# Splitting the projection matmuls of a two-layer hybrid trunk into halves of 256 columns

## The chip, the cores and the metric

The kernel runs on one core of a Trainium2 chip. The metric is the device time of one execution in microseconds (us). A core has a matrix engine (TensorE; PE in the profile, its weight loads PEld), a vector engine (DVE), a scalar engine (ACT), GpSimd (POOL) and a sync engine (SP) that issues most of the transfers.

## What is computed

512 tokens of 1,024 features pass two layers. Each layer normalizes its input, projects it to a wide row (queries, keys, values, gate), mixes the tokens, multiplies by the gate and projects back:

```python
for i in range(2):
    mod = silu(c) @ ada_w[i] + ada_b[i]
    shift, scale, gate = split(mod, 3)
    h = rms_norm(x, norm_g[i]) * (1 + scale) + shift
    if i == 0:   # retention, 4 heads; w_in is 1024 x 6144
        q, k, v, g = split(h @ ret_w_in, ...)
        o = rms_norm(retention(rope(q), rope(k), v)) * silu(g)
        out = o @ ret_w_out
    else:        # chunked attention, 16 heads; w_in is 1024 x 8192
        q, k, v, g = split(h @ att_w_in, 4)
        o = attention(rms_norm(q), rms_norm(k), v, bias) * silu(g)
        out = o @ att_w_out
    x = x + gate * out
```

The arithmetic is float32. The kernel gets it from TensorE with three products: each operand is split into a high and a low part, and high x high, high x low and low x high are summed.

## The kernel before, in words

**Input projections.** A `Chunk` (L290) is 512 columns of `w_in` (256 in one case at the start). Its weights come in two halves of 512 rows: `load` (L248) transfers them to `raw`, and ACT and DVE split them into `whi` and `wlo`. `Chunk.unit` then issues, for 128 tokens or 128 features and one half of the rows, 4 k-tiles of 3 matmuls into one PSUM tile `pm_...`; the second half ends the sum, and `evac` takes it. There are two forms:

- `nat_mm` (L270): the activations `hT` are the stationary operand (128 columns of it), 512 columns of weights stream past; L275 to L277. Used for `pm_rv` (values of layer 0), `pm_aqk` (queries and keys of layer 1) and `pm_av` (values). The output projections `po_r` and `po_a` use it as well.
- `tr_mm` (L279): the weights are stationary and 512 tokens of `hT` stream past; L283 to L285. Used for `pm_rqk`, `pm_rg` and `pm_ag` (queries and keys of layer 0, the gates).

A PSUM tile holds 128 x 512 float32. Every matmul of the program loads its stationary operand itself.

**Other products.** The scores `st` (L586, layer 0) and `as` (L787, layer 1) and the mixings `ro` (L606) and `ao` (L827) have 512, 384 or 256 columns, since later tokens see more keys; those of 256 are whole matmuls, not halves. A mixing block has twelve matmuls, three of 512, three of 384 and six of 256. Transposes (`hp`, `qt`, `pt`, `ss`) and column sums (`mod`) have 128 columns or one.

**The order.** Products run as units of 12 matmuls, one after the other in the order of the `go(...)` calls; scores, transposes, mixings and the adaLN sums of the next layer (`acc`, L150, on DVE) are hung behind given units with `at`. A planner in the framework sets the final order of each engine by simulated times. At the start (L386 to L464) the adaLN vectors of layer 0 are built from their weights by quarters, and the first products run beside that, k-tiles at a time.

Of the kernel before, what the change touches and what calls it, by code (L numbers as in the profile page):

```python
# [17 lines left out]
P = 128  # L18
S = 512
# [23 lines left out]
def hybrid_trunk_kernel(  # L43
# [71 lines left out]
    def rstd_of(ss, n, w):  # L115
        """ss [P, w] sums of squares over n -> (ss / n + eps) ** -0.5."""
        ms = sp.tile([P, w], F32, tag="ms", name="ms")
        nc.gpsimd.tensor_scalar(ms, ss, 1.0 / n, EPS, ALU.mult, ALU.add)
        rs = sp.tile([P, w], F32, tag="rs", name="rs")
        nc.gpsimd.tensor_tensor(rs, ms, mhalf[:, :w], ALU.pow)  # L120
        return rs

# [1 line left out]
    def ada_load(pool, layer, col, half):  # L124
# [9 lines left out]
    def ada_acc(pool, layer, col):  # L134
        """sum over k-tiles of cond * ada_w on every partition: [P, 512], in two steps;
        a gate's bias stands in the sum of the first partition."""
        acc = np_.tile([P, 512], F32, tag="acc", name=f"acc_{layer}_{col}", bufs=1)
        gate = col >= 2 * D
        if gate:
            nc.gpsimd.memset(acc, 0.0)  # L140
            nc.gpsimd.dma_start(acc[0:1, :], ada_b[layer : layer + 1, col : col + 512])
        for half in range(2):
            raw = ada_load(pool, layer, col, half)
            for k in range(4):
                kt = half * 4 + k
                c1 = cond[:, kt : kt + 1]
                if kt == 0 and not gate:
                    nc.vector.tensor_scalar(acc, raw[:, k, :], c1, None, ALU.mult)
                else:
                    nc.vector.scalar_tensor_tensor(acc, raw[:, k, :], c1, acc, ALU.mult, ALU.add)  # L150
            if half == 0:
                yield
        yield acc

    def column_sums(blocks, name, direct=False):
        """blocks: lists of [P, P]; the sums over their partitions, as [P, blocks]."""
        n, z = len(blocks), len(blocks[0])
        if direct:
            ps = pa.tile([P, n], F32, tag="pa", name=name)
            for j, parts in enumerate(blocks):  # L160
                for i, a in enumerate(parts):
                    mm = nc.tensor.matmul(
                        ps[:, j : j + 1], a, ones[:, 0:1], start=i == 0, stop=i == z - 1
                    )
            return ps, mm
        ps = pa.tile([P, n, z * P], F32, tag="pa", name=name)
        for j, parts in enumerate(blocks):
            for i, a in enumerate(parts):
                mm = nc.tensor.transpose(ps[:, j, i * P : (i + 1) * P], a, ident)
        sums = sp.tile([P, n], F32, tag=f"sums{n}", name=f"sums_{name}")  # L170
        nc.vector.tensor_reduce(sums, ps, mybir.AxisListType.X, ALU.add)
        return sums, mm

    def ada_finish(layer, col, accs, n):
        """n * 128 columns of scale or shift, summed over the partitions and laid over them."""
        c0 = col // P
# [12 lines left out]
    def ada(pool, layer, col):  # L189
        """512 columns: scale and shift laid over the partitions, the gate on each of them."""  # L190
        for acc in ada_acc(pool, layer, col):
# [13 lines left out]

# [1 line left out]
    def norm_rows(t, tag, scalar=False):  # L207
        """x / rms(x), in two halves of the columns."""
        xn, ss = [], sp.tile([P, 2], F32, tag="ss", name=f"ss_{tag}_{t}")
# [36 lines left out]

# [1 line left out]
    def load(parts, name, width=512, scale=None, w=None, k0=0, k1=4, low=None):  # L248
        """k-tiles k0..k1 of a piece of 4; parts: (columns of the tile, rows of the weights)."""
        if w is None:  # L250
# [18 lines left out]

    def nat_mm(ps, ah, al, tsl, w, kt0, first, last, ks=range(4)):  # L270
        """ps[tok, 512] += a[k, tok]^T w[k, 512]: ah/al(k) give the activations."""
        _, wh, wl = w
        for k in ks:
            a_h, a_l = ah(kt0 + k)[:, tsl], al(kt0 + k)[:, tsl]
            nc.tensor.matmul(ps, a_h, wh[:, k, :], start=first and k == 0, stop=False)  # L275
            nc.tensor.matmul(ps, a_h, wl[:, k, :], start=False, stop=False)  # L276
            nc.tensor.matmul(ps, a_l, wh[:, k, :], start=False, stop=last and k == 3)  # L277

    def tr_mm(ps, csl, w, kt0, first, last, ks=range(4)):  # L279
        _, wh, wl = w  # L280
        for k in ks:
            h, l = hT["h"][:, kt0 + k, :], hT["l"][:, kt0 + k, :]
            nc.tensor.matmul(ps, wh[:, k, csl], h, start=first and k == 0, stop=False)  # L283
            nc.tensor.matmul(ps, wh[:, k, csl], l, start=False, stop=False)  # L284
            nc.tensor.matmul(ps, wl[:, k, csl], h, start=False, stop=last and k == 3)  # L285

# [3 lines left out]
    class Chunk:  # L290
        """Columns of an input projection; cols: list of (columns of the tile, first column)."""

# [15 lines left out]
        def unit(self, half, u, ks=range(4)):  # L308
            if half == 0 and ks[0] == 0:
                self.ps.append(  # L310
                    self.pool.tile([P, 512], F32, tag=self.tag, name=f"pm_{self.name}_{u}")
                )
            sl = slice(u * P, (u + 1) * P)
            if self.transposed:
                tr_mm(self.ps[u], sl, self.w, half * 4, half == 0, half == 1, ks)
            else:
                nat_mm(self.ps[u], hh, hl, sl, self.w, half * 4, half == 0, half == 1, ks)
            if half == 1 and ks[-1] == 3:
                self.evac(u, self.ps[u])
# [10 lines left out]

    # Products run as units of 12 matmuls; the other work is hung behind given units.
    now = [0]
# [52 lines left out]

# [1 line left out]
    new_h(0)  # L387
# [5 lines left out]
    with tc.tile_pool(name="st", bufs=1) as st:  # L393
# [42 lines left out]
        def prepare(s, behind=None):  # L436
            """features 256 * s.. of h, and their rows of the first weights."""
            ada_256(D + s * 256, "scale", s == 0, behind)
# [29 lines left out]
    def probabilities(pool):  # L468
        """key tiles j on the partitions, their queries from tile j on; the last one is
        given the tile before it, as zeros."""  # L470
        pth = pool.tile([P, 1408], F32R, name="pth")
# [6 lines left out]

    # ================= layer 0: retention =================
    with ExitStack() as l0:  # L480
# [116 lines left out]
        def mix(n, f):  # L597
            """a block of 128 features of head n: products, gate and gain; the mean square waits."""
            ps = pa.tile([P, 512], F32, tag="pa", name=f"ro_{n}_{f}")
# [18 lines left out]
            nc.vector.tensor_tensor(y, ps, gg[n, f], ALU.mult)  # L618
            # the last head takes the place of the queries and keys, which are done with
            a, b = ("yh", "yl") if n < 3 else (("qh", "ql"), ("kh", "kl"))[f % 2]  # L620
# [9 lines left out]
        def norm_y(n):  # L630
            """1 / rms of head n for each token, on the partitions."""
            ps, _ = column_sums([[rstd[n][:, t * P : (t + 1) * P]] for t in range(NT)], f"ss_{n}")
# [61 lines left out]
        new_h(1)  # L694
        # the first weights of layer 1 take the place of the last values
        early = Chunk("aqk0", att_w_in, qk_cols(0), False, None)
# [7 lines left out]

    # ================= layer 1: chunked attention =================
    with ExitStack() as l1:
# [5 lines left out]
        def do_qk(b, begun=None):  # L712
            """heads 2b, 2b + 1."""
            nat = []
# [120 lines left out]
        def finish(h):  # L835
# [4 lines left out]
            else:  # L840
                if not last_y:
                    # the last heads take the place of the layer's input
                    last_y["h"] = hp.tile([P, NK, S], F32R, tag="hTh", name="yh_last")
# [5 lines left out]
        def hang(h, a, b, c, d=0):  # L849
            """behind units: a the scores, b the transposes, c the mixing."""  # L850
            at(a - 3, bias, h)
# [46 lines left out]
def _constants():  # L898
    """Tables that depend on shapes alone: rope frequencies and retention decays."""
    inv = np.array([int(v, 16) for v in _INV_FREQ_HEX.split()], dtype=np.uint32).view(np.float32)  # L900
# [66 lines left out]
```

## Time and profile before

| | |
|---|---|
| time, median of 2 runs | 999.24 us (996.72 and 1,001.76) |
| span of the profiled execution | 996.1 us |
| TensorE matmuls | 963.9 us busy (97%), 4,572 instructions |
| TensorE weight loads | 803.9 us (81%), 4,572 instructions |
| DVE | 608.7 us (61%) |
| ACT | 384.3 us (39%) |
| POOL | 212.1 us (21%) |
| DMA | 111.26 MB, mean 112 GB/s |

The span runs from the first to the last instruction of one profiled execution. Busy time is the union of the records of an engine; matmul records overlap, so a listed duration is longer than the distance between the starts of two neighbours. "Releaser" is what ended an idle time.

### The profile page before, as it was taken

The numbers are of one execution on the slowest core, as the hardware profiler recorded it, in microseconds if no ns is written. First come the engines' busy times: TensorE is split into PE (matmuls) and PEld (weight loads), VectorE is DVE, ScalarE is ACT, GpSimd is POOL, SyncE is SP. The second block draws the span as 40 slices with busy tenths as digits, with TensorE's granted clock in tenths as the row PEclk, the third lists the DMA queues.
The fourth block names the chain that finished last, engine by engine and source line by source line (L and its number), as shares of the span: only waits on it lengthen the run. The fifth ranks groups of instructions, "written<-read, shape, count | busy, mean of one in ns | idle before, by whom it ended". The sixth has DMA issues, their size and how long they took to land.

```text
span 996.1 us, 11965 instructions
## 1 busy us (share of the span) xinstructions
PE 963.9 (97%) x4572; PEld 803.9 (81%) x4572; DVE 608.7 (61%) x1012; ACT 384.3 (39%) x813; POOL 212.1 (21%) x205
## 2 busy tenths in 40 slices
PE   4999979999999999999999999999999999999988
PEld 3778868888778888888788888888888888888876
DVE  6977789558862563766445566545556346556683
ACT  6433413232223333426344445234543244444431
POOL 4810231004200103612100270002520012004520
PEclk8799989999999999999999999999999999999999
DMA  9645534653262222222232222223223232213202
GB/s 336 215 129 188 180 126 129 193 196 124 89 209 98 85 85 84 85 85 85 93 104 71 74 96 96 96 85 93 73 78 97 84 96 90 90 56 99 91 1 85
DMA packets 80537, 111.26 MB, mean 112 GB/s; under 512 B 12016, under 2 KB 44832, under 8 KB 80480
## 3 DMA queue, kind: packets, MB, share of 16 engines
q1 hardware_dynamic: 68368, 102.77, 31.3%
q0 software_dynamic: 10960, 5.63, 2.1%
q10 hardware_dynamic: 1152, 2.10, 0.6%
q8 instruction: 36, 0.59, 0.2%
q14 instruction: 21, 0.17, 0.1%
HBM read 108.32 MB, written 2.10 MB: 111 GB/s over the span
## 4 chain that ended last, share of the span: by engine, by line
PE 81%; DVE 8%; DMA 5%; issue 3%; POOL 1%; ACT 1%; SPq 0%; POOLq 0%; DVEq 0%; ACTq 0%
PE pm_aqk L277 6%; PE pm_aqk L275 6%; PE pm_aqk L276 6%; PE ao L827 3%; PE as L787 3%; PE pm_av L276 3%; PE pm_av L277 3%; PE pm_av L275 3%; PE po_a L277 3%; PE po_a L276 3%; PE po_a L275 3%; PE pm_ag L283 3%; DVE acc L150 3%; PE pm_ag L284 3%; PE pm_ag L285 3%; DMA ada<-in_ada_w_dram 3%
## 5 line engine op out<-in xcount | busy, mean ns | idle before, releaser
L275 PE MATMUL pm_aqk<-whi_aqk,hTh 128*128 128x512 f32 x256 | 101.8, 398 | 0.0
L277 PE MATMUL pm_aqk<-whi_aqk,hTl 128*128 128x512 f32 x256 | 100.5, 393 | 0.0
L276 PE MATMUL pm_aqk<-wlo_aqk,hTh 128*128 128x512 f32 x256 | 100.3, 392 | 0.0
L150 DVE SCALAR_TENSOR_TENSOR acc<-ada,cond,acc 128x512 f32<-128x512 f32 x60 | 52.9, 882 | 22.5 <-DMA ada<-in_ada_w_dram 11.5
L275 PE MATMUL pm_rv<-whi_rv,hTh 128*128 128x512 f32 x128 | 52.3, 413 | 5.4 <-ACT hTh L350 5.4
L277 PEld LDWEIGHTS pm_aqk<-whi_aqk,hTl 128*128 128x128 f32 x256 | 48.1, 188 | 10.1
L775 POOL DMA_DIRECT2D br<-in_att_bias_dram x16 | 13.4, 837 | 200.3 <-DVE nm L794 172.1
L275 PEld LDWEIGHTS pm_aqk<-whi_aqk,hTh 128*128 128x128 f32 x256 | 48.1, 188 | 9.5
L276 PEld LDWEIGHTS pm_aqk<-wlo_aqk,hTh 128*128 128x128 f32 x256 | 48.2, 188 | 9.3
L267 DVE TENSOR_TENSOR wlo_aqk<-raw_aqk,whi_aqk 128x2048 fp32r<-128x2048 f32 x16 | 36.6, 2289 | 30.3 <-ACT whi_aqk L266 30.3
L796 ACT ACTIVATE p<-p,nm 128x128 f32<-128x128 f32 (+1 forms) x64 | 35.9, 563 | 49.3 <-DVE nm L794 48.3
L263 POOL TENSOR_TENSOR raw_r<-raw_r,gate 128x2048 f32<-128x2048 f32 x8 | 39.5, 4937 | 72.1 <-DMA raw_r<-in_ret_w_out_dram 70.5
L275 PE MATMUL po_r<-whi_r,yh 128*128 128x512 f32 x128 | 51.8, 407 | 1.5 <-DVE rt L532 1.5
L790 DVE CUSTOM_DVE_ANT_0 p<-as,br 128x128 f32<-128x128 f32 (+1 forms) x64 | 30.4, 486 | 36.8 <-PE as L787 33.9
L276 PE MATMUL pm_rv<-wlo_rv,hTh 128*128 128x512 f32 x128 | 52.4, 409 | 0.0
L276 PE MATMUL po_r<-wlo_r,yh 128*128 128x512 f32 x128 | 51.7, 404 | 0.0
L277 PE MATMUL po_r<-whi_r,yl 128*128 128x512 f32 x128 | 51.6, 403 | 0.0
L285 PE MATMUL pm_rqk<-hTh,wlo_rqk 128*128 128x512 f32 x128 | 49.7, 391 | 1.8 <-DVE wlo_rqk L267 1.8
L283 PE MATMUL pm_ag<-hTh,whi_ag 128*128 128x512 f32 x128 | 50.7, 398 | 0.0
L283 PE MATMUL pm_rqk<-hTh,whi_rqk 128*128 128x512 f32 x128 | 50.7, 397 | 0.0
L284 PE MATMUL pm_ag<-hTl,whi_ag 128*128 128x512 f32 x128 | 50.4, 394 | 0.0
L277 PE MATMUL pm_rv<-whi_rv,hTl 128*128 128x512 f32 x128 | 50.3, 401 | 0.0
(219 smaller groups left out, 2622.3 us busy)
## 6 DMA issues: line engine op xcount, KB each, us to landing
ada<-in_ada_w_dram SPq DMA_DIRECT2D x16, 1024.0 KB, 5.1
raw_aqk<-in_att_w_in_dram SPq DMA_DIRECT2D x32, 512.0 KB, 4.6
ada<-in_ada_w_dram SPq DMA_DIRECT2D x16, 512.0 KB, 8.4
raw_rg<-in_ret_w_in_dram SPq DMA_DIRECT2D x8, 1024.0 KB, 5.1
raw_r<-in_ret_w_out_dram SPq DMA_DIRECT2D x8, 1024.0 KB, 5.0
raw_ag<-in_att_w_in_dram SPq DMA_DIRECT2D x8, 1024.0 KB, 5.4
raw_av<-in_att_w_in_dram SPq DMA_DIRECT2D x8, 1024.0 KB, 5.3
raw_a<-in_att_w_out_dram SPq DMA_DIRECT2D x8, 1024.0 KB, 5.1
```

What stands on the lines that cost most here:

```text
L150: nc.vector.scalar_tensor_tensor(acc, raw[:, k, :], c1, acc, ALU.mult, ALU.add)
L263: nc.gpsimd.tensor_tensor(raw, raw, scale.unsqueeze(1).broadcast_to([P, k1 - k0, width]), ALU.mult)
L267: (low or nc.vector).tensor_tensor(lo, raw, f32(hi), ALU.subtract)
L275: nc.tensor.matmul(ps, a_h, wh[:, k, :], start=first and k == 0, stop=False)
L276: nc.tensor.matmul(ps, a_h, wl[:, k, :], start=False, stop=False)
L277: nc.tensor.matmul(ps, a_l, wh[:, k, :], start=False, stop=last and k == 3)
L283: nc.tensor.matmul(ps, wh[:, k, csl], h, start=first and k == 0, stop=False)
L284: nc.tensor.matmul(ps, wh[:, k, csl], l, start=False, stop=False)
L285: nc.tensor.matmul(ps, wl[:, k, csl], h, start=False, stop=last and k == 3)
L787: nc.tensor.matmul(ps[:, :w0], a[:, qsl], b[:, :w0], start=z == 0, stop=z == 2)
L790: nc.vector.tensor_tensor_reduce(p[:, :w], ps[:, :w], br[:, S - w :], 1.0, -3.0e38, ALU.add, ALU.max, mx)
L796: nc.scalar.activation(p[:, :w], p[:, :w], AF.Exp, bias=nm, accum_out=sm)
```

## The change

Each of the three matmuls of a k-tile is issued as two, over columns 0 to 255 and 256 to 511, with the same stationary operand, one right after the other. This holds for `tr_mm` and for `nat_mm` where `Chunk.unit` calls it; the output projections call `nat_mm` without `halves` and keep 512 columns. The flag that starts a sum is set on the first half of the first matmul alone, the one that ends it on the last half of the last. The other hunks of the diff take out comments.

```diff
-    def nat_mm(ps, ah, al, tsl, w, kt0, first, last, ks=range(4)):
+    def nat_mm(ps, ah, al, tsl, w, kt0, first, last, ks=range(4), halves=False):
         _, wh, wl = w
+        n0 = 256 if halves else 512
         for k in ks:
             a_h, a_l = ah(kt0 + k)[:, tsl], al(kt0 + k)[:, tsl]
-            nc.tensor.matmul(ps, a_h, wh[:, k, :], start=first and k == 0, stop=False)
-            nc.tensor.matmul(ps, a_h, wl[:, k, :], start=False, stop=False)
-            nc.tensor.matmul(ps, a_l, wh[:, k, :], start=False, stop=last and k == 3)
+            for z, (a, b) in enumerate(((a_h, wh), (a_h, wl), (a_l, wh))):
+                for n in range(0, 512, n0):
+                    nc.tensor.matmul(
+                        ps[:, n : n + n0], a, b[:, k, n : n + n0],
+                        start=first and k == 0 and z == 0 and n == 0,
+                        stop=last and k == 3 and z == 2 and n + n0 == 512,
+                        skip_group_check=halves,
+                    )

     def tr_mm(ps, csl, w, kt0, first, last, ks=range(4)):
         _, wh, wl = w
         for k in ks:
             h, l = hT["h"][:, kt0 + k, :], hT["l"][:, kt0 + k, :]
-            nc.tensor.matmul(ps, wh[:, k, csl], h, start=first and k == 0, stop=False)
-            nc.tensor.matmul(ps, wh[:, k, csl], l, start=False, stop=False)
-            nc.tensor.matmul(ps, wl[:, k, csl], h, start=False, stop=last and k == 3)
+            for z, (a, b) in enumerate(((wh, h), (wh, l), (wl, h))):
+                for n in range(0, S, 256):
+                    nc.tensor.matmul(
+                        ps[:, n : n + 256], a[:, k, csl], b[:, n : n + 256],
+                        start=first and k == 0 and z == 0 and n == 0,
+                        stop=last and k == 3 and z == 2 and n > 0,
+                        skip_group_check=True,
+                    )

         # in Chunk.unit
-                nat_mm(self.ps[u], hh, hl, sl, self.w, half * 4, half == 0, half == 1, ks)
+                nat_mm(self.ps[u], hh, hl, sl, self.w, half * 4, half == 0, half == 1, ks, True)
```

## Rows read from the trace of the kernel before

**Rows 1.** The page: span, engines (busy us, share, instructions), chain's shares by engine

```profile
span 996.1 us, 11965 instructions
...
PE 963.9 (97%) x4572; PEld 803.9 (81%) x4572; DVE 608.7 (61%) x1012; ACT 384.3 (39%) x813; POOL 212.1 (21%) x205
...
PE 81%; DVE 8%; DMA 5%; issue 3%; POOL 1%; ACT 1%; SPq 0%; POOLq 0%; DVEq 0%; ACTq 0%
```

**Rows 2.** Windows: stretch, its us, busy us (instructions) by engine, clock, DMA share, GB/s

```profile
0.00:60.00 60.00, 43.16 (x190) 36.19 (x191) 44.14 (x85) 32.56 (x68) 34.76 (x54) 0.86 0.74 256
60.00:142.50 82.50, 76.86 (x362) 64.07 (x360) 65.73 (x86) 28.45 (x37) 12.26 (x10) 1.00 0.44 143
500.00:600.00 100.00, 100.00 (x491) 84.05 (x490) 53.33 (x118) 44.11 (x128) 24.64 (x24) 1.00 0.26 82
```

**Rows 3.** Chain that ended last, 60 to 150 us: shares by line

```profile
by line: DMA ada<-in_ada_w_dram 28.8%; DVE acc L150 20.9%; issue 11.9%; DVE rt L532 6.5%; DMA acc<-in_ada_b_dram 4.8%; DVE wlo_rqk L267 3.8%; DVE wlo_rg L267 2.9%; PE po_r L275 2.7%; DVE wlo_r L267 2.5%; DVE ang L509 2.2%; PE po_r L276 2.2%
```

**Rows 4.** Groups by line, shapes kept apart: form, count, busy us, mean ns, idle before

```profile
L275 PE MATMUL pm_aqk<-whi_aqk,hTh 128*128 128x512 f32 x256 | 101.8, 398 | 0.0
...
L275 PE MATMUL pm_av<-whi_av,hTh 128*128 128x512 f32 x128 | 50.0, 391 | 0.0
...
L733 PEld LDWEIGHTS qt<-ident,qn 128*128 128x128 f32 x128 | 15.4, 140 | 3.9 <-DVE qn L725 1.3
```

**Rows 5.** Timeline of TensorE: start us, us; first projection of a stretch and the 97th

```profile
637.37 0.39 PE L275 MATMUL pm_av<-whi_av,hTh 128*128 128x512 f32 x1
...
659.13 0.39 PE L275 MATMUL pm_aqk<-whi_aqk,hTh 128*128 128x512 f32 x1
```

**Rows 6.** Timeline of TensorE in the start, two neighbours

```profile
25.46 0.63 PE L277 MATMUL pm_rv<-whi_rv,hTl 128*128 128x512 f32 x1
25.89 0.63 PE L275 MATMUL pm_rv<-whi_rv,hTh 128*128 128x512 f32 x1
```

**Rows 7.** Timeline of TensorE, a mixing and scores of layer 1

```profile
797.57 0.39 PE L827 MATMUL ao<-pth,vh 128*128 128x512 f32 x1
...
798.25 0.33 PE L827 MATMUL ao<-pth,vh 128*128 128x384 f32 x1
...
798.77 0.29 PE L827 MATMUL ao<-pth,vh 128*128 128x256 f32 x1
798.90 0.28 PE L827 MATMUL ao<-ptl,vh 128*128 128x256 f32 x1
...
799.49 0.28 PE L787 MATMUL as<-kh,qh 128*128 128x256 f32 x1
...
800.21 0.40 PE L275 MATMUL pm_aqk<-whi_aqk,hTh 128*128 128x512 f32 x1
```

**Rows 8.** Timeline of TensorE, scores of layer 0: the first, and what follows the sixth

```profile
103.60 0.28 PE L586 MATMUL st<-qh,kh 128*128 128x256 f32 x1
...
104.31 0.40 PE L606 MATMUL ro<-pth,vh 128*128 128x512 f32 x1
```

**Rows 9.** Timeline of TensorE, a mixing of layer 0 and what follows it

```profile
315.00 0.40 PE L606 MATMUL ro<-pth,vh 128*128 128x512 f32 x1
...
315.70 0.34 PE L606 MATMUL ro<-pth,vh 128*128 128x384 f32 x1
...
316.22 0.28 PE L606 MATMUL ro<-pth,vh 128*128 128x256 f32 x1
...
316.91 0.40 PE L283 MATMUL pm_rg<-hTh,whi_rg 128*128 128x512 f32 x1
```

**Rows 10.** Timeline of the weight loads: six of transposes, and two of scores

```profile
700.32 0.68 PEld L733 LDWEIGHTS qt<-ident,qn 128*128 128x128 f32 x6
...
799.85 0.19 PEld L787 LDWEIGHTS as<-kl,qh 128*128 128x128 f32 x1
799.97 0.19 PEld L787 LDWEIGHTS as<-kh,ql 128*128 128x128 f32 x1
```

## The prediction

> **What bounds the kernel now.** I read the page first: TensorE's matmuls are busy for 963.9 of 996.1 us, and 81% of the chain that ended last is TensorE [rows 1]. Then the windows: from 500 to 600 us TensorE is busy for all 100 us at clock 1.00 [rows 2]. So a nanosecond more per matmul there is a nanosecond at the end. Two stretches differ. Up to 60 us TensorE is busy for 43.2 us at a mean clock of 0.86, and from 60 to 142.5 us it is idle for 82.5 - 76.9 = 5.6 us [rows 2], and there the chain runs over the loads of the adaLN weights and the vector engine's sums of them (L150), not over products [rows 3]. What TensorE loses there can vanish in the waits.
>
> **What the change does to the instructions.** The two helpers issue the products of 18 groups (six projections by three lines): three groups of 256 for pm_aqk and fifteen of 128 for the others, one of each shown [rows 4]: 3 x 256 + 15 x 128 = 2,688 matmuls of 512 columns. They become 5,376 of 256. Columns, sums, DMAs and evacuations stay. Each matmul brings its own weight load: both counts on the page are 4,572 [rows 1], although L275 and L276 already use the same stationary tile one after the other. So I count on 2,688 added loads also.
>
> **What a matmul of 512 columns costs.** Its listed duration (391 to 398 ns) [rows 4] is not its cost, since records overlap; the cost is the distance between starts. In the longest even stretch 96 projection matmuls go from 637.37 to 659.13 us: 21.76 / 96 = 226.7 ns [rows 5]. In the slow part of the start two neighbours are 0.43 us apart [rows 6], which is 512 columns at 1.2 GHz, one a cycle (that this is the low level I take from the number and the mean clock of that stretch). At 2.4 GHz the columns alone would take 213.3 ns; so 13.4 ns of the 226.7 are something else.
>
> **What a half will cost.** Everything hangs on whether these 13.4 ns belong to the matmul or to its columns. If to the matmul, a half costs 106.7 + 13.3 = 120 ns and a pair 240, 13.3 more than now. If to the columns, a half costs 113.3 ns and a pair what one costs now. The trace has matmuls of 256 columns, each with its own load, in the scores and mixings:
> - layer 1: six of ao from 798.77 to 799.49 and six of as from there to 800.21, 0.72 us each: 120 ns. The three of 512 columns in that ao block take 0.68 us (227 ns), as the projections do [rows 7].
> - layer 0 scores: six from 103.60 to 104.31, 118 ns [rows 8].
> - layer 0 mixing: six from 316.22 to 316.91, 115 ns [rows 9]. But its three of 512 before it take 0.70 us, 233 ns.
>
> By whole blocks the fixed part wins: the twelve matmuls of a mixing have 3 x (512 + 384) + 6 x 256 = 4,224 columns, 1,760 ns at 2.4 GHz. By matmul that makes 1,760 + 12 x 13.3 = 1,920 ns, by columns 4,224 / 512 x 226.7 = 1,870. Measured: 1.92 us in layer 1 [rows 7] and 1.91 in layer 0 [rows 9]. I take 120 ns, since in ao the 512-column matmuls run at the projections' own 227. The bounds are 113.3 ns below (columns only; the layer 0 mixing comes near it) and 130 above, the slowest visible step of a half (798.77 to 798.90) [rows 7]. Below 113.3 there is little room: six transposes' weight loads of 0.14 us each [rows 4] take 0.68 us together [rows 10], so (0.68 - 0.14) / 5 = 108 ns from load to load, where only 128 columns are streamed.
>
> The Trainium skill, "Perfetto Trace Analysis", section "Identifying the Most-Contended Engine", has one judge TensorE by the busy share of LDWEIGHTS. Here that is 81%, and 2,688 more of 0.188 us would be 505 us on top of 803.9, over the span. By the trace they would not add so: loads listed at 0.19 us start 0.12 us apart [rows 10], so the records overlap and the listed time is no price; a time over the 1,309 us of the two sums I hold for nearly excluded (under 0.01, left in the chance of the third rival).
>
> **The sum.** Up to 60 us there are 190 matmuls and from there to 142.5 us 362 [rows 2]; by the names pm_ in the timeline 106 and 278 of them are projections. The first lie amid waits and partly at the low clock, where 256 columns take just half of 0.43 us. The second would cost 278 x 13.3 = 3.7 us, against 5.6 us of idle there [rows 2]: hidden; without that cover 3.7 us more. The other 2,304 lie where TensorE has no idle time to give: 2,304 x 13.3 ns = 30.7 us. The work that waits on the products (evacuations, splits, softmax) is paced by TensorE and only gains slack; vector engine 53.3 and scalar engine 44.1 of 100 us [rows 2]. The weights' transfers are issued as before. The span goes from 996.1 to 1,026.8 us. The median of the runs (999.2) lies 3.1 us over the span, so I forecast 1,030.
>
> **Rivals.**
> 1. *The forecast:* a half at 118 to 120 ns. With 118, 2,304 x (236 - 226.7) = 21 us: 1,021. With 120 and nothing hidden, 2,688 x 13.3 = 36 us: 1,035. Chance 0.60.
> 2. *No change (the other side):* a half costs half, the 13.4 ns being columns. For it: the layer 0 mixing at 115, and within that run the later steps at 0.11 to 0.12 us; against it: as and ao. At 113.3 the time is 999, at 115 it is 999.2 + 2,304 x 3.3 ns = 1,007. It decides from a half below 117.7 ns, where 2,304 pairs cost under 20 us (2%). The Trainium skill, "TensorE: Matmul & The Clock Gate", section "Wait — 56ns, not 53.3ns?", gives about 2.5 ns of fixed cost for a warm matmul; by that the sum would be 2,304 x 2.5 = 5.8 us, 1,005. The trace's 13.4 ns over the columns does not agree with it. Chance 0.26.
> 3. *Slower still:* no run here has more than about a dozen halves in a row. Over thousands, loading or issuing may fall behind the streaming, with no long matmul between to catch up. With 125 to 130 ns a half: 2,304 x (250 to 260 - 226.7) = 54 to 77 us: 1,053 to 1,076. For it: a load every 108 ns where little is streamed [rows 10] leaves only some 5 ns of reserve beside 113. Against it: as holds 120 evenly. Chance 0.10.
> 4. *Faster:* halves at the load's own 108 to 109 ns would give 2,304 x 8.7 ns = 20 us back: 979. Nothing streams 256 columns that fast in this trace. Chance 0.04.
>
> **Numbers.** About 2% is what a measurement of this kernel can tell from no change. Case 1 is nearly all over that, case 2 under it. Faster 0.04, same 0.27, slower 0.69. The likeliest case's own range is 1,019 to 1,036. To hold 8 in 10 the range must take in most of case 2, so it goes from 998 to 1,042, which leaves out rivals 3 and 4 and a little of 2.
>
> **What would show it.** In the profile after: 5,376 matmuls under pm_, 7,260 in all with as many loads; in the even stretch of pm_av near 640 us (some 25 us later by then) starts 120 ns apart, not 113; the stretch before 142 us hardly longer than now; the same 233 ns in po_r and the same as, ao, st as now. If starts are 113 to 115 apart, the step from "per matmul" to "per column" was wrong; if they are 125 and more in long runs but not in short ones, rival 3 holds. If matmuls of 256 columns lack their own load, the count was wrong. A different order of the work, which the planner may choose since there are more instructions, could move waits about by some us; the wait before 142 us and the last softmax are where I'd see it.

## The result and the profile after

| | before | after |
|---|---|---|
| median | 999.24 us | 1,035.55 us (1,034.54 and 1,036.56) |
| ratio | | 1.0372 (95% interval 1.033 to 1.0415) |
| span of the profiled execution | 996.1 us | 1,032.8 us |
| TensorE busy | 963.9 us | 992.4 us |
| TensorE idle (span less busy) | 32.2 us | 40.4 us |

Slower by 3.7%. The page after, span and busy time by engine, answers to [rows 1]:

```profile
span 1032.8 us, 17325 instructions
...
PE 992.4 (96%) x7260; PEld 944.4 (91%) x7260; DVE 625.8 (61%) x1012; ACT 385.0 (37%) x813; POOL 207.4 (20%) x205
```

The counts are those foretold: 7,260 matmuls and as many loads. The span has grown by 36.7 us, of which 28.5 are busy time and 8.2 idle time of TensorE. The even pace is in the timeline of TensorE (a row merges the two halves of a matmul):

```profile
663.14 0.40 PE L278 MATMUL pm_av<-whi_av,hTh 128*128 128x256 f32 x2
...
664.82 0.40 PE L278 MATMUL pm_av<-wlo_av,hTh 128*128 128x256 f32 x2
```

Seven pairs in 1.68 us: 240 ns a pair, 120 ns a half, against 226.7 for the whole matmul in [rows 5]. Over 2,688 pairs that is 35.8 us; not all of it reaches the end, since the start hides some. The windows (columns as in [rows 2]) and the first product that follows the start:

```profile
0.00:60.00 60.00, 42.75 (x315) 41.34 (x316) 43.83 (x87) 32.57 (x68) 35.45 (x54) 0.94 0.75 259
60.00:150.00 90.00, 84.78 (x641) 82.02 (x640) 74.35 (x93) 30.64 (x40) 20.14 (x11) 0.98 0.47 153
150.00:490.00 340.00, 338.08 (x2400) 317.69 (x2399) 208.81 (x257) 112.63 (x173) 61.10 (x43) 1.00 0.36 115
490.00:1032.80 542.80, 526.81 (x3910) 503.33 (x3909) 298.85 (x577) 209.17 (x533) 90.69 (x97) 1.00 0.26 80
```

```profile
145.02 0.39 PE L278 MATMUL po_r<-whi_r,yh 128*128 128x512 f32 x1
```

Before, the first output projection started at 144.0 us, and windows of the kernel before show the stretch around it and all that follows:

```profile
144.01 0.77 PE L275 MATMUL po_r<-whi_r,yh 128*128 128x512 f32 x1 [1.28 <-DVE rt L532]
```

```profile
142.50:152.00 9.50, 8.22 (x26) 6.39 (x24) 9.50 (x13) 1.23 (x2) 5.39 (x1) 0.64 0.57 221
150.00:996.10 846.10, 837.61 (x4008) 698.89 (x4006) 491.37 (x830) 322.03 (x706) 161.59 (x141) 1.00 0.30 97
```

The first output projection starts at 145.0 us and not at 144.0, so of 384 x 13.3 = 5.1 us up to there only 1 us came through. The granted clock had a part in this: up to 60 us its mean was 0.94, where it had been 0.86 [rows 2], and around the first output projections it was 1.00 (142.5 to 152 us) where it had been 0.64, most of it at the lower level, 1.2 GHz: the neighbours at 144.57 and 145.00 us were 0.43 us apart, behind waits of TensorE of 3.9 and 1.3 us. From 150 us on the stretch has grown from 846.1 to 882.8 us: TensorE's busy time by 27.3 us (837.6 to 864.9), its idle time by 9.4 (8.5 to 17.9). In the last window TensorE is idle for 542.8 - 526.8 = 16.0 us. Waits of TensorE from 480 us on, after and then before:

```profile
PE as L798 <- DVE ptl L362: 5.3, 4, 3.2
PE pt L818 <- DVE p L810: 3.6, 3, 1.5
PE qt L744 <- DVE qn L736: 2.4, 1, 2.4
```

```profile
PE as L787 <- DVE ptl L351: 2.5, 1, 2.5
PE qt L733 <- DVE qn L725: 0.9, 1, 0.9
```

Before there were two such waits, 3.4 us; after there are eight, 11.3 us. One of them in the timeline: a transpose of the probabilities stands in the middle of a gate unit, and TensorE waits for the softmax (DVE L810):

```profile
608.23 0.40 PE L291 MATMUL pm_ag<-hTh,whi_ag 128*128 128x256 f32 x2
610.12 0.33 PE L818 MATMUL pt<-ident,p 128*128 128x128 f32 x1 [1.49 <-DVE p L810]
```

The planner has ordered the work anew for the doubled instructions, and this order waits more; whether the order alone is the reason is a question for the experiments.

### The profile page after: what moved, and what is told of

Read it like the earlier page. It is cut to its first block, busy times and chain, and to the rows that moved or that the text cites. A ratio compares the mean times of both kernels' runs of the same rounds, so it can differ in the third digit from the quotient of the medians.

```text
span 1032.8 us, 17325 instructions
## 1 busy us (share of the span) xinstructions
PE 992.4 (96%) x7260; PEld 944.4 (91%) x7260; DVE 625.8 (61%) x1012; ACT 385.0 (37%) x813; POOL 207.4 (20%) x205
## 3 DMA queue, kind: packets, MB, share of 16 engines
q10 hardware_dynamic: 1152, 2.10, 0.5%
## 5 line engine op out<-in xcount | busy, mean ns | idle before, releaser
L278 PE MATMUL pm_aqk<-whi_aqk,hTh 128*128 128x256 f32 x512 | 105.1, 285 | 0.0
L278 PE MATMUL pm_aqk<-whi_aqk,hTl 128*128 128x256 f32 x512 | 104.0, 284 | 0.0
L278 PE MATMUL pm_aqk<-wlo_aqk,hTh 128*128 128x256 f32 x512 | 103.9, 284 | 0.0
L786 POOL DMA_DIRECT2D br<-in_att_bias_dram x16 | 13.4, 839 | 243.8 <-DVE nm L805 210.1
L150 DVE SCALAR_TENSOR_TENSOR acc<-ada,cond,acc 128x512 f32<-128x512 f32 x60 | 50.0, 833 | 13.9 <-DMA acc<-in_ada_b_dram 5.4
L278 PE MATMUL pm_rv<-whi_rv,hTh 128*128 128x256 f32 x256 | 52.9, 289 | 4.3 <-ACT hTh L361 4.3
L801 DVE CUSTOM_DVE_ANT_0 p<-as,br 128x128 f32<-128x128 f32 (+1 forms) x64 | 30.7, 487 | 39.3 <-PE as L798 38.8
L291 PE MATMUL pm_ag<-hTh,wlo_ag 128*128 128x256 f32 x256 | 53.6, 286 | 0.0
L291 PE MATMUL pm_ag<-hTl,whi_ag 128*128 128x256 f32 x256 | 53.1, 285 | 0.0
L291 PE MATMUL pm_rg<-hTh,whi_rg 128*128 128x256 f32 x256 | 52.1, 284 | 1.0 <-ACT whi_rg L266 1.0
L291 PE MATMUL pm_rqk<-hTh,whi_rqk 128*128 128x256 f32 x256 | 52.7, 288 | 0.0
L278 PE MATMUL pm_rv<-wlo_rv,hTh 128*128 128x256 f32 x256 | 52.5, 286 | 0.0
L291 PE MATMUL pm_ag<-hTh,whi_ag 128*128 128x256 f32 x256 | 52.3, 285 | 0.0
```

Source lines behind the costliest of these rows:

```text
L278: nc.tensor.matmul(ps[:, n : n + n0], a, b[:, k, n : n + n0], start=first and k == 0 and z == 0 and n == 0, stop=last and k == 3 and z == ...
L291: nc.tensor.matmul(ps[:, n : n + 256], a[:, k, csl], b[:, n : n + 256], start=first and k == 0 and z == 0 and n == 0, stop=last and k == 3 ...
L786: nc.gpsimd.dma_start(br, bass.AP(att_bias.tensor, h * 1280 + 127, [[576, 2], [-1, 64], [1, S]]))
L801: nc.vector.tensor_tensor_reduce(p[:, :w], ps[:, :w], br[:, S - w :], 1.0, -3.0e38, ALU.add, ALU.max, mx)
```

## Experiments

Three questions: are the 36 us the halves or the planner's order, does it matter which operand is stationary, and what are the 13.3 ns?

**The planner taken out of both kernels.** One argument of the framework, in the kernel before and in the changed one:

```diff
-    with tile.TileContext(nc, schedule_with_timeline_sim=True) as tc:
+    with tile.TileContext(nc, schedule_with_timeline_sim=False) as tc:
```

> The kernel before without the planner: each engine's instructions in the order in which the program gives them. It is the base for the next run alone. No theory gives its time from rows; between 990 and 1,040 us I would not be surprised. Needed of it: its span, its idle time of TensorE, and starts 226.7 ns apart in long stretches of projections.

> The changed kernel without the planner. Its order of the products is nearly that of the run before it, so that only the halving differs. Theory (13.3 ns per added matmul, and about 8 us of the measured 36 from the planner's new order): 29 to 33 us over the run without halves, TensorE's idle time within 2 us of it. Rival 1 (the 8 us of idle come with longer products, whatever the order): 36 to 40 us over it, idle time 6 us or more larger. Rival 2 (most of the 36 us is the order): under 15 us over it.

Measured: 1,054.27 us whole (over the 990 to 1,040 that would have been no surprise) and 1,087.37 us in halves, 33.1 us apart. The pages, whole and then halves:

```profile
PE 981.1 (93%) x4572; PEld 811.2 (77%) x4572; DVE 612.7 (58%) x1012; ACT 384.0 (36%) x813; POOL 202.4 (19%) x205
```

```profile
PE 1016.3 (93%) x7260; PEld 963.4 (88%) x7260; DVE 614.7 (56%) x1012; ACT 384.3 (35%) x813; POOL 201.6 (18%) x205
```

With nearly the same order in both, TensorE's busy time grows by 35.2 us and its idle time by 3.1 (72.5 to 75.6, from spans of 1,053.6 and 1,091.9 us; the profiled execution of the halves, 1,093.7 us, was the longest of four). Of the 38.3 us between the spans, 13.0 lie ahead of the first output projection (at 154.6 and 167.6 us), where the clock differs too: 1.00 and 0.85 from 120 to 155 us. Behind it busy time grows by 28.7 us and idle time shrinks by 3.4. So most of the loss is the halves, and the rival that idle time grows by 6 us or more whatever the order finds no support. The difference of the medians, 33.1, is just over the upper edge of what the theory gave, and the idle time of the whole span just over its 2 us.

**One form alone.** `nat_mm` in halves and `tr_mm` whole, and the other way round:

```diff
 # nat_only: tr_mm as before
-            for z, (a, b) in enumerate(((wh, h), (wh, l), (wl, h))):
-                for n in range(0, S, 256):
+            nc.tensor.matmul(ps, wh[:, k, csl], h, ...)   # and the two others, 512 columns
 # tr_only: in Chunk.unit
-                nat_mm(..., half == 0, half == 1, ks, True)
+                nat_mm(..., half == 0, half == 1, ks)
```

> Halves only where the activations are stationary (768 matmuls of pm_aqk, 384 of pm_rv, 384 of pm_av: 1,536). Theory: 1,536 x 13.3 ns = 20.4 us less what the start hides, plus whatever the planner's order for this kernel costs (0 to 8 us): 1,015 to 1,027. Rival (the stationary weights of the other form are what is dear): under 1,007.

> Halves only where the weights are stationary (pm_rqk, pm_rg, pm_ag: 1,152). Theory: 1,152 x 13.3 ns = 15.3 us less what the start hides, plus the planner's order (0 to 8 us): 1,011 to 1,022. Rival (this form carries the cost): 1,027 and more. Rival (it carries none): under 1,004.

Measured: 1,026.13 us (ratio 1.0286, 1.0249 to 1.0323) and 1,019.37 us (1.0218, 1.0193 to 1.0244), beside 997.25 before; both lie in the range that the theory gave. The pages' busy time:

```profile
PE 981.5 (96%) x6108; PEld 884.4 (87%) x6108; DVE 617.6 (60%) x1012; ACT 385.0 (38%) x813; POOL 205.3 (20%) x205
```

```profile
PE 977.8 (96%) x5724; PEld 866.4 (85%) x5724; DVE 620.3 (61%) x1012; ACT 382.6 (38%) x813; POOL 211.9 (21%) x205
```

Busy time grows by 17.6 us for 1,536 matmuls and 13.9 for 1,152: 11.5 and 12.1 ns for each, so both forms pay alike. TensorE's idle time is 39.3 and 38.7 us (spans 1,020.8 and 1,016.5), 7 us over that of the kernel before in either. About half of the added matmuls bring nearly as many waits as all of them (8.2 us). This speaks for the new order as their reason, and against the number of halves.

**The output projections too.** `n0 = 256` in every call of `nat_mm`.

> The changed kernel with the output projections in halves also (768 matmuls more, po_r and po_a). Theory (the cost belongs to the matmul): po_a goes from 227 to 240 ns a pair (384 x 13.3 = 5.1 us), po_r from 233 to 240 (384 x 6.7 = 2.6 us): 1,043 us, give or take what the planner's new order does (5 us). Rival (a pair of halves costs what one costs, and the planner's order was the reason): 1,036 or less, and starts in po_a 113 ns apart.

Measured: 1,038.81 us (1.0408, 1.0376 to 1.044), 3 us over the change where 7.7 were expected. TensorE's busy time grows by 5.2 us (992.4 to 997.6). In `po_a` a half costs 120 ns, but in `po_r` 113 to 118 ns, so a pair costs no more than the 233 ns that a whole one of `po_r` takes. By the timeline of this run, seven matmuls of `po_r` in halves:

```profile
151.49 0.39 PE L278 MATMUL po_r<-whi_r,yh 128*128 128x256 f32 x2
...
153.08 0.39 PE L278 MATMUL po_r<-wlo_r,yh 128*128 128x256 f32 x2
```

1.59 / 7 = 227 ns a pair. A fixed 13.3 ns for each matmul does not allow that.

**Other cuts.** The same code with other borders:

```diff
-                for n in range(0, 512, n0):
+                for n, n0 in [(0, 384), (384, 128)]:     # or 288 + 224, or four of 128
```

> As the changed kernel, but cut into 384 and 128 columns instead of 256 and 256. Two theories of the 13.3 ns. Per matmul: the pair costs 240 ns again (173.3 + 66.7), so 1,036 us. Load-bound (a matmul can start no sooner than some 110 to 120 ns after the one before it, since its weights begin to load only then, and 120 ns in the halves is that bound): 173 + 110 to 120 = 283 to 293 ns a pair, 45 to 55 ns over the halves, so 2,304 to 2,688 pairs make 1,140 to 1,180 us. If 128 columns of this type are streamed more slowly than 256 for a reason of their own, the starts behind them are further apart than 120 ns.

> As the changed kernel, but cut into 288 and 224 columns. Per matmul: 133.3 + 106.7 = 240 ns a pair, so 1,036 us. Load-bound: 133 + 113 to 120 = 246 to 253 ns, so 1,052 to 1,071 us. Read from the starts: behind a matmul of 224 columns the next starts after 107 ns (per matmul) or not before 113 to 120 (load-bound).

> Each matmul of the input projections cut into four of 128 columns. Per matmul: 4 x 66.7 = 266.7 ns for 512 columns, 40 more than whole: 2,688 x 40 = 107 us, 1,105 us. Load-bound: 4 x 110 to 120 = 440 to 480 ns, 213 to 253 more: 1,570 to 1,680 us.

Measured, one execution each: 1,147.72, 1,045.44 and 1,652.18 us. The first and the third lie where the load-bound theory put them and 110 and 550 us over the other. The timeline of TensorE, 384 and 128 columns (each row is one of 384 with the one of 128 behind it), and of the loads beside it:

```profile
699.82 0.45 PE L291 MATMUL pm_ag<-hTl,whi_ag 128*128 128x384 f32 x2
700.11 0.45 PE L291 MATMUL pm_ag<-hTh,wlo_ag 128*128 128x384 f32 x2
700.39 0.45 PE L291 MATMUL pm_ag<-hTh,whi_ag 128*128 128x384 f32 x2
```

```profile
700.05 0.30 PEld L291 LDWEIGHTS pm_ag<-hTh,wlo_ag 128*128 128x128 f32 x2
700.34 0.30 PEld L291 LDWEIGHTS pm_ag<-hTh,whi_ag 128*128 128x128 f32 x2
```

A pair takes 0.285 us, not 0.240. The loads come two at a time: the second of two starts 0.30 - 0.19 = 0.11 us after the first, and the next two start 0.29 - 0.11 = 0.18 us after that, about what 384 columns take (173 ns in `ao`, [rows 7]). Quarters, four to a row:

```profile
999.77 0.61 PE L278 MATMUL pm_aqk<-whi_aqk,hTh 128*128 128x128 f32 x4
1000.22 0.61 PE L278 MATMUL pm_aqk<-wlo_aqk,hTh 128*128 128x128 f32 x4
```

0.45 us for four, 112 ns for a matmul that streams only 128 columns. It is close to the 108 ns from load to load in [rows 10]. The cut into 288 and 224 is the finest test of the three. Its time, 1,045, is below the 1,052 that load-bound began with. Its timeline and its page:

```profile
640.41 0.41 PE L291 MATMUL pm_ag<-hTl,whi_ag 128*128 128x288 f32 x2
...
642.86 0.41 PE L291 MATMUL pm_ag<-hTh,wlo_ag 128*128 128x288 f32 x2
```

```profile
PE 1010.1 (97%) x7260; PEld 963.0 (92%) x7260; DVE 616.7 (59%) x1012; ACT 384.7 (37%) x813; POOL 204.7 (20%) x205
```

Ten pairs in 2.45 us are 245 ns a pair. Busy time is 17.7 us over the changed kernel's, 6.6 ns a pair, which makes 246.6 ns: at the lower edge of load-bound's 246 to 253, where per matmul it would be 240 again. But the sign that the expectation named did not come: behind a matmul of 224 columns the next one starts after 98 to 108 ns in most cases, not after 113 to 120, and it is the one of 288 that takes longer than its columns, 139 to 148 ns. Whether a recorded start is the moment in which the columns begin to stream is not shown. Idle time is 33.6 us (the span is 1,043.7), 6.8 less than in the changed kernel, in another order and with longer products.

**The place of the activations.** In the kernel before, the stationary operands of `po_r` and `ro` start 64 bytes off a multiple of 128 in each partition, since two small tiles lie ahead of them; those of layer 1 and of the projections start on one. This is worked out from the sizes of the tiles; no trace shows addresses. The activations moved, nothing else; in `nat_mm` they are the stationary operand, in `tr_mm` the one that streams:

```diff
     def new_h(layer):
+        if layer == 0:
+            hp.tile([P, 16], F32, name="pad_0")
         hT["h"] = hp.tile([P, NK, S], F32R, tag="hTh", name=f"hTh_{layer}")
         hT["l"] = hp.tile([P, NK, S], F32R, tag="hTl", name=f"hTl_{layer}")
+        if layer == 0:
+            hp.tile([P, 16], F32, name="pad_1")
```

> The kernel before with 64 bytes of unused memory in each partition ahead of the activations hT and 64 behind them: hT starts 64 bytes off a multiple of 128, the weights stay on one; the order of all engines stays as it is. In all runs so far the products of layer 0 whose stationary operand lies so (po_r, ro) take 233 ns for 512 columns, where those of the projections take 227, and 113 to 118 for 256 columns where the projections' halves take 120. Theory (the place decides): the projections take 233 ns, 2,304 to 2,688 x 6.6 ns = 15 to 18 us more than before: 1,012 to 1,015. Rival (the place has nothing to do with it): 997, as before.

> The changed kernel with the same shift of hT. Theory (the place decides): halves start 113 to 118 ns apart, a pair takes some 231 ns instead of 240: 2,688 x 9 ns = 24 us less than the changed kernel, 1,012 us, and no slower than whole matmuls with the same shift but for the 8 us of waits that this order has (0 to 10 us more). Rival (13.3 ns for each matmul, wherever its operands lie): 1,036, as the changed kernel.

Measured: 1,005.25 us whole (1.0063, 1.0037 to 1.009) and 1,023.54 us in halves (1.0246, 1.0213 to 1.028), beside 1,000.37 before. Both move the way that was expected, and both by less: whole matmuls lose 5 us and not 15 to 18, halves gain 12 us on the changed kernel's 1,035.55 and not 24. Halves were to be at most 10 us slower than whole ones here; they are 18 us slower. The order of all engines is that of the unshifted kernels. The timeline of the halves, two stretches, and of the whole ones, one:

```profile
504.90 0.39 PE L295 MATMUL pm_ag<-hTh,whi_ag 128*128 128x256 f32 x2
...
511.48 0.39 PE L295 MATMUL pm_ag<-hTh,wlo_ag 128*128 128x256 f32 x2
```

```profile
524.52 0.40 PE L282 MATMUL pm_av<-whi_av,hTh 128*128 128x256 f32 x2
...
525.70 0.40 PE L282 MATMUL pm_av<-whi_av,hTl 128*128 128x256 f32 x2
```

```profile
378.23 0.39 PE L287 MATMUL pm_rg<-hTh,whi_rg 128*128 128x512 f32 x1
...
380.79 0.39 PE L289 MATMUL pm_rg<-hTh,wlo_rg 128*128 128x512 f32 x1
```

29 pairs in 6.58 us are 113 ns a half, five in 1.18 us are 118: the pace is 113 in some stretches and 118 in others, in either form, where it was 120 before the shift. The whole ones of `pm_rg` take 2.56 / 11 = 233 ns, as expected, but those of `pm_av`, where the moved activations are stationary, only 229 (nine in 2.06 us from 510.61 us on). So the larger effect came where the moved operand streams: the place of the stationary operand alone does not decide. What a half costs beyond its columns depends on where the operands lie. Why the same 64 bytes make whole matmuls slower and halves faster is open.

**Operands of two bytes.** The projections read the upper halves of the same float32 words:

```diff
+def top(ap):
+    return ap.bitcast(BF16)[:, 1::2]
-                        ps[:, n : n + n0], a, b[:, k, n : n + n0],
+                        ps[:, n : n + n0], top(a), top(b[:, k, n : n + n0]),
```

> The projections' operands are read as bfloat16, the upper two bytes of each float32 (so the low parts of the product are kept only in bfloat16): whole matmuls of 512 columns, same counts and bytes apart. If the 13.3 ns come with operands of four bytes, starts are 213 to 217 ns apart, 2,304 x 10 to 13 ns = 23 to 31 us less than before: 966 to 975 us. If they come with every matmul, 227 ns and 997 us.

> The same with halves of 256 columns. If the 13.3 ns come with operands of four bytes: 107 to 111 ns a half, 214 to 222 a pair, within 10 us of the whole ones read as bfloat16 apart from the planner's waits. If with every matmul: 120 ns, 30 us and more over the whole ones.

Measured, one execution each: 999.26 and 1,009.98 us. TensorE is busy for 956.0 and 960.1 us: halving costs 4 us of busy time here, where with four bytes it costs 28.5. The other 6.5 us of the difference are idle time (41.5 and 48.1 us). The timeline of the halves, that of the whole ones, and the halves' load as a group (mean ns behind the busy us):

```profile
640.08 0.39 PE L283 MATMUL pm_av<-whi_av,hTl 128*128 128x256 bf16 x2
...
640.98 0.39 PE L283 MATMUL pm_av<-whi_av,hTh 128*128 128x256 bf16 x2
```

```profile
642.61 0.39 PE L283 MATMUL pm_av<-whi_av,hTl 128*128 128x512 bf16 x1
...
645.99 0.39 PE L283 MATMUL pm_av<-whi_av,hTl 128*128 128x512 bf16 x1
```

```profile
L283 PEld LDWEIGHTS <-hTh 128*128 128x128 bf16 x2048 | 194.9, 97 | 44.6 <-issue 5.8 <-ACT hTh L366 4.5
```

Four pairs in 0.90 us: 112.5 ns a half by these rounded rows. Fifteen whole matmuls of the other run take 3.38 us, 225 ns each. So with two-byte operands two halves cost what one whole costs, and the whole costs nearly what it costs with four. The expectation had joined two things wrongly: the 13.4 ns of the whole matmul stay (they do not come with operands of four bytes), but a half has only half of them. A load is listed with 97 ns here; with four bytes it is this, in the changed kernel:

```profile
L278 PEld LDWEIGHTS pm_aqk<-whi_aqk,hTh 128*128 128x128 f32 x512 | 80.2, 191 | 0.8
```

## Why the prediction was right, and where it was not

- *The price of a half, 120 ns:* right, to the nanosecond in the even stretches. It had been read from `as` and `ao` [rows 7], which had the same type of operands.
- *The reason, a fixed 13.3 ns for each matmul:* wrong. This was the step "by whole blocks the fixed part wins". The 13.4 ns of a whole matmul go with its columns: two-byte halves take half of the whole, 113 ns. A fixed cost would make a pair of 384 and 128 columns cost 240 ns and four quarters 267; they cost 285 and 450. These two fit another rule: a matmul costs what is longer, its columns (about 0.443 ns each, 226.7 / 512) or a weight load of 112 ns. That gives 170 + 112 = 282 and 4 x 112 = 448. The whole matmul has 227 ns for its load. Close to the edge the rule gives too little: 128 + 112 = 240 for 288 and 224, measured 245, and 113.3 for a half, measured 120. These 7 ns went away with two-byte operands, whose load is listed with half the time, so the load is their likely reason. It is not shown: in that run the streamed operand was of two bytes too, and 64 bytes in the place of the activations took 2 to 7 ns off. The price had been read from rows of the same shape; that it equalled 106.7 + 13.3 was luck, and the twelve matmuls of a block came out nearly the same by either account. In layer 0 the block's sum agreed because three of 512 columns at 233 ns made up for six of 256 at 115. The third rival had the mechanism in a sentence (some 5 ns of reserve), but put its price above 120.
- *That the load begins only when the matmul before has started*, so that a short matmul delays the next one, fits the two loads 0.11 us apart in the cut of 384 and 128; it is argued from that, not shown.
- The Trainium skill, "TensorE: Matmul & The Clock Gate", section "LDWEIGHTS (loading the stationary operand)", gives a load's time as its columns divided by 1.2, in ns; for 128 columns this makes an estimate of 106.7 ns. The trace nearly agrees: 112 ns from load to load in quarters, not the listed 191. The same page, section "Weight-path perf modes — Fast Weight Load (FWL) and DoubleRow", has a faster load for 128 columns of types other than FP32. The trace agrees: 97 against 191 ns listed, and halves cost 4 us of busy time and not 28.5.
- *The start hides its part:* right in the outcome: 384 pairs lie ahead of the first output projection, 5.1 us, and it came 1.0 us later. The idle time that was to cover it gave only part: from 60 to 150 us it went from 90.0 - 83.1 = 6.9 to 5.2 us. The higher granted clock gave back some of the rest; that was luck, since nothing in the prediction foresaw it.
- *2,304 pairs at 13.3 ns, 30.7 us:* nearly right for the size: from 150 us on TensorE's busy time grew by 27.3 us. The time grew by 36.7 us there; the other 9.4 are idle time.
- *The planner might move waits about by some us:* it did, by 8 us of TensorE's idle time, which the sum had left out. I had looked for it before 142 us and in the last softmax; most of it came in the middle of layer 1, where scores and transposes stand ahead of what they wait for. In the pair without the planner idle time behind the start did not grow, and the two kernels with one form alone have 7.1 and 6.5 of the 8.2 us with about half of the halves; both speak for the order as the reason.
- *Other groups as before:* `po_r` still takes 233 ns and `po_a` 227. The span of 1,026.8 that the sum gave was 6 us short.

## What to carry to other kernels

Read the cost of a matmul from the distance of starts, and ask for each shape whether columns or load set it: with four-byte operands and 128 stationary columns, a matmul of 256 columns sits on the edge (120 ns, where its columns alone would be 113), so whole 512 columns leave the load room and cutting them cost 13 ns a pair. A price read from rows of the same shape and type can be right while its explanation is wrong; one run with another size tells. Where a planner sets the order, a change of the instruction count can cost by the new order as well, some 8 of 36 us here; compare both kernels without the planner before blaming the instructions.

## What the runs showed that was not expected

- 64 bytes in the place of the activations, stationary in one form and streamed in the other, changed a half from 120 to 113 or 118 ns, and the whole kernel by +5 us (whole) or -12 us (halves).
- Whole matmuls of 512 columns take 224 to 227 ns with two-byte operands also, 5 to 6% more than the columns at 2.4 GHz (213.3). What takes it was not found.
- Idle time of TensorE varied between 28.9 and 48.1 us in planned kernels with the same 2,688 products whole or in pairs: 32.2 whole, 28.9 with 384 + 128 columns, 33.6 with 288 + 224, 40.4 with 256 + 256, 48.1 with halves of two-byte operands. The order is not all of it: with the order of the changed kernel unchanged, it was 44.6 us where the moved activations made the halves faster.
